# Experts' matmuls in two passes behind a branch on the token count, a gather of whole rows, and a share of the weight split for GpSimd

## The chip, the cores and the metric

The kernel runs on one core of a Trainium2 chip. The metric is the device time of one execution in microseconds: 1957.58 us, the median of three runs (1957.22 to 1958.94). The core has five engines that work side by side and wait for each other through semaphores: TensorE (PE, matmuls), VectorE (DVE), ScalarE (ACT), GpSimd (POOL) and SyncE (SP), which here only issues DMA transfers.

## The reference

Two encoder layers, each with a token mixer, a cross-attention and a channel mixer, over 256 tokens of width 1024, all in float32. The channel mixer of the second layer is a mixture of eight experts, and it is the part that the change touches:

```python
def moe_swiglu(x, w_router, w_gate, w_up, w_down):
    logits = (xt @ w_router).astype(jnp.float32)
    top_logit, top_e = lax.top_k(logits, TOP_K)          # TOP_K = 2 of 8
    top_w = jax.nn.softmax(top_logit, axis=-1)
    ...
    def expert_block(args):
        xs, e = args
        hdn = jax.nn.silu(xs @ w_gate[e]) * (xs @ w_up[e])
        return hdn @ w_down[e]
```

`w_gate[e]` and `w_up[e]` are 1024 x 3584, `w_down[e]` is 3584 x 1024. With the inputs given, the router sends 79, 52, 30, 59, 51, 63, 92 and 86 tokens to experts 0 to 7: five of the eight have at most 64.

## The kernel before

**Split numbers.** Every float32 operand is held as two parts, a high one `h` (the number rounded to the matmul's format) and a low one `l` (the rest). A product takes three passes on PE: high x high, high x low weights, low x high weights.

**Weights.** `wload` brings 1 MB of a weight (a piece: 128 partitions x 2048 columns) through SP's queue into a buffer `wr` (11 of them in the expert stage: 2 + 5 + `NX` = 3, and one more from the cross-attention), and takes it apart into `wh` and `wl`: ACT copies with rounding (`wh`, L312), and DVE subtracts (`wl = wr - wh`, L316). Outside the token mixer DVE does all of the subtraction, in `PX` = 4 parts of 512 columns in the expert stage. In the token mixer a part of the columns goes to POOL (L319). `wh` and `wl` live in a ring of 4 pairs of buffers.

**An expert.** `gather` takes the tokens of an expert into 128 slots: matmuls of `xtok` (both parts) against a selection `pd` give x^T of the expert in PSUM, and ACT copies it into `xg`. `expert_run` then walks 7 chunks of 512 hidden columns. For each, `gate_up` loads four pieces (gate twice, up twice) and runs 2 x 8 x 3 matmuls of 512 columns; SiLU on ACT and a product on DVE make `hs`. `down` of the chunk before follows: four transposes, the split into `hh` and `hl`, two pieces, and 24 matmuls into `ps_ye`. So a chunk has six pieces, an expert 42, and the stage 336 pieces and 8 x 504 such matmuls. `combine` adds the weighted result into `x`. Behind the stage a branch on the largest count (L1463) skips a second run for experts with over 128 tokens; it is skipped with these inputs.

**Order.** One program order, in which a scheduler of the tile framework moves instructions ahead where buffers allow. Each engine then works strictly in its own order. SP issues the loads in that order too; a load waits until DVE has read the last of what the buffer held.

Of the kernel before, what the change touches and what calls it, by code (L numbers as in the profile page):

```python
# [10 lines left out]
F32 = mybir.dt.float32  # L11
# [8 lines left out]
P = 128  # L20
# [17 lines left out]
PM, PC, PX = 2, 4, 4  # L38
# [6 lines left out]
NX = 3  # L45
# [13 lines left out]
GQ = 16  # L59
LEVELS = (16, 8, 4, 2, 1)  # L60
# [61 lines left out]
def _tiles():  # L122
    """name -> (index, first k-tile, k-tiles, first column, columns) of the pieces in which a weight is loaded"""
# [39 lines left out]
def tile_encoder(ctx: ExitStack, tc: tile.TileContext, a: dict, out: bass.AP, cw: dict):  # L163
# [95 lines left out]
    def load_rest(M):  # L259
# [10 lines left out]
        # lower bound of the second layer  # L270
# [19 lines left out]
    where = _offsets()  # L290

    def wload(name, i, k0, n0, c0, n1, late=()):
        """late: instructions behind which the parts are taken"""
# [8 lines left out]
        # behind a norm only the first weights may be split before it ends  # L302
# [3 lines left out]
        with ExitStack() as es:  # L306
# [3 lines left out]
            g = n * (GQ - GP[layer[0]]) // GQ if in_mixer[0] else n  # L310
            for s in (slice(j, j + c) for j in range(0, n, c)):
# [11 lines left out]
    def wload_halves(name, i, k0, n0, c0, n1, cols):  # L323
        """a piece of weights as two halves of its columns or of its k-tiles, in small buffers"""
# [19 lines left out]
    def together(*parts):  # L344
        """interleaves generators that yield the share of their work that is done"""
# [9 lines left out]
    def later(gen, n):  # L355
        """the steps of a generator as if they stood n instructions further down"""
# [13 lines left out]
    def proj_feat_steps(name, i, c0, ncol, xh, xl, evac, bank_=None):  # L370
        """out^T[f, tok]: weights stationary"""
# [38 lines left out]
    def rms_rstd(dst, ss, n, bias=None):  # L410
        """dst = (ss / n + eps) ** -0.5"""
# [15 lines left out]
    def log_sig(dst, src):  # L427
        """dst = ln(1 + exp(-src)) = -ln(sigmoid(src))"""
# [7 lines left out]
    def mixer(l, xh, xl, kctx):  # L436
        wi = ("w_in", l)
        with tc.tile_pool(name=f"mx{l}", bufs=1, reuse_waits="tile") as M, ExitStack() as mctx:
# [32 lines left out]
            def unit(f0, n):  # L471
                """l2 norm of the heads of conv tiles f0 .. f0 + n"""
# [10 lines left out]
            def products(w, f0):  # L483
                """k of a chunk against its tiles f0 .. f0 + 3, heads of either parity in a bank"""
# [11 lines left out]
            def A1():  # L496
# [28 lines left out]
                # (I + L^T)^-1 of the 32-blocks: 96 blocks side by side on the partitions  # L525
# [34 lines left out]
            def A1c(LT, wm):  # L560
# [37 lines left out]
            def A1b(beta, ld, DB):  # L598
# [38 lines left out]
            def A2(k_t, v_t, beta, ef, cdp, fb, AT, U64, col_b):  # L637
                # u', w'^T, k decays
# [37 lines left out]
                # state recurrence  # L676
# [30 lines left out]
                # outputs  # L707
# [76 lines left out]
            # C projections  # L784
# [97 lines left out]
    def softmax_rows(M, ps, n, scale, pt):  # L882
        """ps [P, n, 256] logits in PSUM -> pt [P, n, 256] probabilities"""
# [62 lines left out]
    def mixer_c(l, MS, big, c2, g2, M, sg, qc, ci, cg, oc):  # L946
# [27 lines left out]
        # chunk decays and the decayed queries  # L974
# [17 lines left out]
        # state recurrence  # L992
# [107 lines left out]
    def affine(e, x, mean, rstd, lp):  # L1100
        """x <- (x - mean) * rstd * gain + bias"""
# [168 lines left out]
    def moe(l, i, xh, xl, xth, xtl):  # L1270
        with weights("r3", NX, ring=raws), tc.tile_pool(name="mo", bufs=1, reuse_waits="tile") as O:
# [19 lines left out]
            # experts ahead of an expert: a larger logit, or the same one and a lower index  # L1291
# [35 lines left out]
            V.tensor_copy(cnti, cnt)  # L1327
            slot2 = sm("slot2")
# [3 lines left out]

            def gather(e, sl):
                pd = O.tile([P, NH, P], F32R, name="pd", tag="pd", bufs=2)
# [4 lines left out]
                for i, src in enumerate((xth, xtl)):  # L1339
                    for k0 in (0, 4):  # L1340
                        pg = bank(psb, "pb", "ps_gt").rearrange("p (k t) -> p k t", k=4)
                        for k in range(4):
                            for hf in range(NH):
                                T.matmul(pg[:, k], src[:, hf, (k0 + k) * P:(k0 + k + 1) * P], pd[:, hf],
                                         start=hf == 0, stop=hf == NH - 1)
                        A.activation(g[:, i, k0:k0 + 4], pg, AF.Copy)
                return g[:, 0], g[:, 1]
# [203 lines left out]
```

## Time and profile before

| | us |
|---|---|
| median of three timed runs | 1957.58 |
| span of the profiled execution (first to last instruction) | 1961.2 |
| first weight subtraction of the expert stage to the end of the last | 926.4 to 1936.5 |

The profiled execution gives no time of its own beside its span, which is 3.6 us over the median of the timed runs. In the views below a row of an engine carries the line of the kernel that made it, what it wrote and read, shapes and times. PE's matmuls are pipelined and their recorded durations overlap, so the distance from one start to the next is their pace.

### The profile page before, as it was taken

Reading aid. Unit: us, or ns where it says so; the run is one execution under the profiler, and the core shown is the slowest. Engines: PE = TensorE matmul, PEld = TensorE weight load, DVE = VectorE, ACT = ScalarE, POOL = GpSimd, SP = SyncE. Lnnn points to the kernel's source line nnn. Section 1 sums busy time; section 2 is a strip of 40 time slices with the busy share of each in tenths; the row PEclk is TensorE's granted clock in tenths of the full one; section 3 lists DMA queues with packets and bytes.
Section 4 is the critical chain, followed back from the end, with each engine's and each line's share of the span. In section 5 each row is a group of like instructions: output and inputs, shape, how many; then the busy total and the mean of one; then the engine's idle time right before and its main releaser. Section 6 shows DMA issues by size and latency. Waiting matters only on the chain. (4 is left out here: it accounts for less than half of the span.)

```text
span 1961.2 us, 31715 instructions
## 1 busy us (share of the span) xinstructions
PE 1838.9 (94%) x11906; PEld 1544.8 (79%) x11906; DVE 1575.2 (80%) x2812; ACT 1277.4 (65%) x2559; POOL 257.4 (13%) x248
## 2 busy tenths in 40 slices
PE   6889999999979898998999999999999999999996
PEld 5778779899967777686888788887888878788784
DVE  7887665755578966665889989899899898998986
ACT  4755435555536544454788778787877877787774
POOL 4545310000036353001000000000000000000000
PEclk8988999999989888998999999999999999999998
DMA  6321255555323313552999999999999989999980
GB/s 217 111 101 67 90 190 206 176 180 185 126 81 119 103 67 108 215 215 95 350 354 354 346 357 342 354 350 350 346 350 354 351 335 358 339 353 343 347 349 23
DMA packets 71266, 473.44 MB, mean 241 GB/s; under 512 B 8768, under 2 KB 12224, under 8 KB 15936
## 3 DMA queue, kind: packets, MB, share of 16 engines
q1 hardware_dynamic: 70384, 466.09, 64.6%
q10 hardware_dynamic: 720, 5.24, 0.7%
q8 instruction: 95, 1.56, 0.3%
q14 instruction: 67, 0.55, 0.1%
HBM read 470.26 MB, written 1.05 MB: 240 GB/s over the span
## 5 line engine op out<-in xcount | busy, mean ns | idle before, releaser
L316 DVE TENSOR_TENSOR wl<-wr,wh 128x512 fp32r<-128x512 f32 (+2 forms) x1622 | 1017.6, 693 | 119.3 <-ACT wh L312 116.8
L312 ACT ACTIVATE wh<-wr 128x512 fp32r<-128x512 f32 (+1 forms) x1656 | 915.0, 630 | 241.1 <-PE ps_gu L1365 152.2
L1364 PE MATMUL ps_gu<-wl,xg 128*128 128x512 f32 x896 | 352.8, 395 | 0.1
L1363 PE MATMUL ps_gu<-wh,xg 128*128 128x512 f32 x896 | 350.9, 397 | 0.0
L1365 PE MATMUL ps_gu<-wh,xg 128*128 128x512 f32 x896 | 350.6, 392 | 0.0
L1364 PEld LDWEIGHTS ps_gu<-wl,xg 128*128 128x128 f32 x896 | 169.0, 189 | 37.8 <-DVE wl L316 2.3
L1363 PEld LDWEIGHTS ps_gu<-wh,xg 128*128 128x128 f32 x896 | 169.1, 189 | 36.8 <-ACT wh L312 0.5
L1365 PEld LDWEIGHTS ps_gu<-wh,xg 128*128 128x128 f32 x896 | 168.8, 188 | 36.9
L1387 PE MATMUL ps_ye<-wh,hh 128*128 128x512 f32 x448 | 176.7, 396 | 4.6 <-ACT hh L408 4.6
L1388 PE MATMUL ps_ye<-wl,hh 128*128 128x512 f32 x448 | 176.6, 394 | 0.0
L1389 PE MATMUL ps_ye<-wh,hl 128*128 128x512 f32 x448 | 169.8, 397 | 0.0
L319 POOL TENSOR_TENSOR wl<-wr,wh 128x384 fp32r<-128x384 f32 (+6 forms) x68 | 103.6, 1544 | 290.4 <-ACT wh L312 290.1
L1475 POOL TENSOR_TENSOR x<-x,lp 128x512 f32<-128x512 f32 x1 | 1.8, 1817 | 1029.2 <-ACT x L1474 1029.2
L1387 PEld LDWEIGHTS ps_ye<-wh,hh 128*128 128x128 f32 x448 | 84.2, 188 | 26.7 <-ACT hh L408 7.9
L1257 PE MATMUL ps_gu<-xTl,wh 128*128 128x256 f32 x352 | 99.1, 282 | 0.0
L1388 PEld LDWEIGHTS ps_ye<-wl,hh 128*128 128x128 f32 x448 | 84.3, 188 | 18.6
L1256 PE MATMUL ps_gu<-xTh,wh 128*128 128x256 f32 x352 | 98.8, 282 | 0.0
L1258 PE MATMUL ps_gu<-xTh,wl 128*128 128x256 f32 x352 | 98.8, 281 | 0.0
L1389 PEld LDWEIGHTS ps_ye<-wh,hl 128*128 128x128 f32 x448 | 82.5, 188 | 17.3
L1257 PEld LDWEIGHTS ps_gu<-xTl,wh 128*128 128x128 f32 x352 | 66.7, 189 | 0.6 <-DVE xTl L408 0.2
L1256 PEld LDWEIGHTS ps_gu<-xTh,wh 128*128 128x128 f32 x352 | 66.7, 190 | 0.5
L1258 PEld LDWEIGHTS ps_gu<-xTh,wl 128*128 128x128 f32 x352 | 66.8, 190 | 0.0
(451 smaller groups left out, 3276.9 us busy)
## 6 DMA issues: line engine op xcount, KB each, us to landing
wr<-in_moe_wg_dram SPq DMA_DIRECT2D x112, 1024.0 KB, 6.8
wr<-in_moe_wu_dram SPq DMA_DIRECT2D x112, 1024.0 KB, 6.9
wr<-in_moe_wd_dram SPq DMA_DIRECT2D x112, 1024.0 KB, 7.0
wr<-in_w_in_dram SPq DMA_DIRECT2D x16, 1024.0 KB, 4.9
wr<-in_ffn_wg_dram SPq DMA_DIRECT2D x11, 1024.0 KB, 5.2
wr<-in_ffn_wu_dram SPq DMA_DIRECT2D x11, 1024.0 KB, 5.0
wr<-in_ffn_wd_dram SPq DMA_DIRECT2D x11, 1024.0 KB, 4.9
wr<-in_xk_dram SPq DMA_DIRECT2D x8, 1024.0 KB, 4.9
```

The lines of the kernel that those rows point to most:

```text
L312: A.activation(h[:, s], raw[:, s], AF.Copy)
L316: V.tensor_sub(l[:, m], raw[:, m], R_(h[:, m]))
L319: G.tensor_sub(l[:, m], raw[:, m], R_(h[:, m]))
L1256: T.matmul(ps[:, g], wh[:, k, fs], xh[:, k, :], start=k == 0, stop=False)
L1257: T.matmul(ps[:, g], wh[:, k, fs], xl[:, k, :], start=False, stop=False)
L1258: T.matmul(ps[:, g], wl[:, k, fs], xh[:, k, :], start=False, stop=k == KT - 1)
L1363: T.matmul(pt, gh[:, k], wh[:, k4], start=k == 0, stop=False)
L1364: T.matmul(pt, gh[:, k], wl[:, k4], start=False, stop=False)
L1365: T.matmul(pt, gl[:, k], wh[:, k4], start=False, stop=k == KT - 1)
L1387: T.matmul(ye[n], hh[:, f0 + f], dh[:, f, ns], start=b, stop=False)
L1388: T.matmul(ye[n], hh[:, f0 + f], dl[:, f, ns], start=False, stop=False)
L1389: T.matmul(ye[n], hl[:, f0 + f], dh[:, f, ns], start=False, stop=z)
```

## The change

Three edits, all in the expert stage, and three constants (`PX` 4 to 2, `NX` 3 to 2, `XPOOL` = 640).

1. *Two passes.* Where an expert has at most 64 tokens, the 64 upper slots of its stationary operand, empty otherwise, hold the low parts of the 64 lower ones (`halves_of`). Two passes then give all three products (and low x low), the upper 64 rows holding the low part's share. For gate and up these rows are folded onto the lower ones by one more matmul with a shifted identity (`fold`), for which ACT copies the product out of PSUM (`fe`); for down, `combine` adds the two rows by its selection matrix. The count is read into a PE register, and each of the 28 groups of products of an expert is written twice, with three passes and with two, behind a compare-and-branch on PE. The copies and folds run for all experts.
2. *Gather of whole rows.* The selection `pd` is stationary, the tokens stream in 512 columns, both parts into one bank; ACT copies the rows out, PE transposes them, and they are split anew.
3. *GpSimd.* Of the 2048 columns of an expert's piece DVE subtracts 1408 (1024 and 384) and POOL 640.

```diff
-PM, PC, PX = 2, 4, 4
+PM, PC, PX = 2, 4, 2
-NX = 3
+NX = 2
+HALF = P // 2
+XPOOL = 640
...
             g = n * (GQ - GP[layer[0]]) // GQ if in_mixer[0] else n
+            if name.startswith("moe"):
+                g = n - XPOOL
...
+            def halves_of(h, l, e):
+
+                t = O.tile([P, 4, HALF], F32, name="t")
+                V.tensor_scalar(t, R_(h)[:, :, HALF:], few[:, 1, e:e + 1], None, op0=OP.mult)
+                V.scalar_tensor_tensor(h[:, :, HALF:], R_(l)[:, :, :HALF], few[:, 0, e:e + 1], t, op0=OP.mult, op1=OP.add)
...
+                many = nc.tensor.value_load(cnti[0:1, e:e + 1], min_val=0, max_val=S) if packs else None
...
+                for n in range(2):
+                    ns = slice(n * 512, n * 512 + 512)
+                    pg = bank(psb, "pb", "ps_gr")
+                    for i, src in enumerate((xth, xtl)):
+                        for hf in range(NH):
+                            T.matmul(pg, pd[:, hf], src[:, hf, ns], start=i + hf == 0, stop=i + hf == NH)
+                    rows = O.tile([P, 512], F32, name="rows", tag="fe", bufs=2)
+                    A.activation(rows, pg, AF.Copy)
...
+                def products(many, ws, h, l):
+
+
+                    def passes(three):
+                        for j, (out, k, wh, wl, b, z) in enumerate(ws):
+                            T.matmul(out, h[:, k], wh, start=b, stop=False)
+                            T.matmul(out, h[:, k], wl, start=False, stop=z and not three)
+                            if three:
+                                T.matmul(out, l[:, k], wh, start=False, stop=z)
+                    if many is None:
+                        passes(True)
+                        return
+                    with tc.If(many > HALF) as c:
+                        passes(True)
+                    with c.Else():
+                        passes(False)
...
+                    if many is not None:
+                        for pt in pgu:
+                            fe = O.tile([P, 512], F32R, name="fe", tag="fe", bufs=2)
+                            A.activation(fe, pt, AF.Copy)
+                            T.matmul(pt, fold[e], fe, start=False, stop=True, skip_group_check=True)
```

DVE, in the middle of the expert stage, before: `wl<-wr,wh` are the weight subtractions (four to a piece), `hs` and `hl` the chunk's own work on what PE left in PSUM, `pd` the selection of the next expert.

```order
L316 TENSOR_TENSOR wl<-wr,wh 128x512 x24
L1369 TENSOR_TENSOR hs<-hs,ps_gu 128x512
L408 TENSOR_TENSOR hl<-ps_hT,hh 128x512
L316 TENSOR_TENSOR wl<-wr,wh 128x512 x8
L408 TENSOR_TENSOR hl<-ps_hT,hh 128x512
L316 TENSOR_TENSOR wl<-wr,wh 128x512 x16
L1369 TENSOR_TENSOR hs<-hs,ps_gu 128x512
L316 TENSOR_TENSOR wl<-wr,wh 128x512 x20
```

DVE at such a place now:

```order
L412 TENSOR_TENSOR hl<-ps_hT,hh 128x512
L1346 TENSOR_SCALAR t<-hh,few 128x256
L1353 TENSOR_SCALAR pd<-consts,slot 128x128 x2
L1392 UNCONDITIONAL_BRANCH
L1347 SCALAR_TENSOR_TENSOR hh<-hl,few,t 128x4x64
L320 TENSOR_TENSOR wl<-wr,wh 128x1024
L320 TENSOR_TENSOR wl<-wr,wh 128x384
```

A piece now has two subtractions on DVE, of 1024 and 384 columns, and the two instructions of `halves_of` have come in (72 of each in the stage).

POOL at the entry of the expert stage, before: the low part of the tokens is its last work until the branch behind the stage (L1446 reads the count for it).

```order
L1106 TENSOR_SCALAR x<-x,mv 128x512
L1107 TENSOR_TENSOR x<-x,lp 128x512
L1108 TENSOR_TENSOR x<-x,lp 128x512
L1215 TENSOR_TENSOR xtokl<-x,xtokh 128x1024 x2
L1446 TENSOR_LOAD cnti
```

POOL at the same place now:

```order
L1111 TENSOR_TENSOR x<-x,lp 128x512
L1112 TENSOR_TENSOR x<-x,lp 128x512
L1219 TENSOR_TENSOR xtokl<-x,xtokh 128x1024 x2
L323 TENSOR_TENSOR wl<-wr,wh 128x640 x4
L1392 UNCONDITIONAL_BRANCH x2
L323 TENSOR_TENSOR wl<-wr,wh 128x640 x3
```

From here POOL has 336 subtractions of 640 columns, one to a piece, where it had none.

PE at a chunk's end, before: the gate product of the next chunk and the down product stand mixed.

```order
L1364 MATMUL ps_gu<-wl,xg 128x512
L1365 MATMUL ps_gu<-wh,xg 128x512
L1375 MATMUL ps_hT<-consts,hs 128x128 x4
L1389 MATMUL ps_ye<-wh,hl 128x512 x2
L1387 MATMUL ps_ye<-wh,hh 128x512
L1388 MATMUL ps_ye<-wl,hh 128x512
```

PE at such a place now:

```order
L1392 UNCONDITIONAL_BRANCH
L1414 MATMUL ps_gu<-fe,fold 128x512 x2
L1392 COMPARE_AND_BRANCH
L1385 MATMUL ps_ye<-wh,hh 128x512
L1386 MATMUL ps_ye<-wl,hh 128x512
L1388 MATMUL ps_ye<-wh,hl 128x512
```

The products now stand in closed groups between branches, twice each, and the folds stand between the groups. The other engines get an unconditional jump at each of the 224 places.

## Rows read from the trace of the kernel before

**Rows 1.** The page's busy times: us, share of the span, instructions.
```profile
PE 1838.9 (94%) x11906; PEld 1544.8 (79%) x11906; DVE 1575.2 (80%) x2812; ACT 1277.4 (65%) x2559; POOL 257.4 (13%) x248
```

**Rows 2.** Busy us by stretch: PE, PEld, DVE, ACT, POOL, PE clock, DMA share, GB/s.
```profile
920.00:940.00 20.00, 16.25 (x74) 14.51 (x72) 15.84 (x51) 11.30 (x23) 2.76 (x2) 0.65 0.60 222
926.40:1936.50 1010.10, 1005.37 (x4603) 824.32 (x4604) 920.29 (x1537) 796.50 (x1506) 0.00 (x0) 0.99 0.91 339
1460.00:1480.00 20.00, 19.52 (x88) 15.41 (x87) 19.96 (x35) 14.89 (x28) 0.00 (x0) 1.00 0.91 340
1860.00:1880.00 20.00, 20.00 (x91) 16.38 (x90) 19.11 (x33) 16.26 (x30) 0.00 (x0) 1.00 1.01 408
```

**Rows 3.** Groups by line, 926.4 to 1936.5: busy us, mean ns | idle before, releasers.
```profile
L316 DVE TENSOR_TENSOR wl<-wr,wh 128x512 fp32r<-128x512 f32 x1344 | 827.8, 685 | 76.3 <-ACT wh L312 74.3 <-DMA wr<-in_moe_wd_dram 1.2
L312 ACT ACTIVATE wh<-wr 128x512 fp32r<-128x512 f32 x1330 | 718.1, 620 | 178.3 <-PE ps_gu L1365 152.2 <-PE ps_ye L1389 24.1 <-ACT hh L408 0.8
L1364 PE MATMUL ps_gu<-wl,xg 128*128 128x512 f32 x896 | 352.8, 395 | 0.1
```

**Rows 4.** Waits of SP's queue: us in total, times, longest.
```profile
SPq L298 <- DVE wl L316: 1321.0, 404, 24.7
```

**Rows 5.** PE in order of time, first and last of a run: start, us.
```profile
1404.52 0.39 PE L1363 MATMUL ps_gu<-wh,xg 128*128 128x512 f32 x1
...
1407.24 0.60 PE L1375 MATMUL ps_hT<-consts,hs 128*128 128x128 f32 x4
```

**Rows 6.** DVE in order of time, first and last weight subtractions of the stage.
```profile
926.40 2.49 DVE L316 TENSOR_TENSOR wl<-wr,wh 128x512 fp32r<-128x512 f32 x4
...
1935.17 1.29 DVE L316 TENSOR_TENSOR wl<-wr,wh 128x512 fp32r<-128x512 f32 x2
```

**Rows 7.** DVE in order of time, in the first layer's mixer.
```profile
26.22 0.47 DVE L460 SCALAR_TENSOR_TENSOR kvs<-cpad,cwt,kvs 128x256 f32<-128x256 f32 x1
26.62 2.96 DVE L316 TENSOR_TENSOR wl<-wr,wh 128x640 fp32r<-128x640 f32 x1
...
43.93 2.75 DVE L513 TENSOR_TENSOR rd<-ld,cmix 128x384 f32<-128x384 f32 x1
...
140.25 0.69 DVE L336 TENSOR_TENSOR hl<-wr,hh 128x512 fp32r<-128x512 f32 x1 [3.21 <-issue]
```

**Rows 8.** POOL in order of time, the same stretches and two more.
```profile
26.41 2.49 POOL L319 TENSOR_TENSOR wl<-wr,wh 128x1024 fp32r<-128x1024 f32 x1 [0.39 <-ACT wh L312]
...
42.22 4.05 POOL L319 TENSOR_TENSOR wl<-wr,wh 128x384 fp32r<-128x384 f32 x2 [5.03 <-ACT wh L312]
...
78.22 1.02 POOL L319 TENSOR_TENSOR wl<-wr,wh 128x384 fp32r<-128x384 f32 x1
...
120.24 2.53 POOL L337 TENSOR_TENSOR hl<-wr,hh 128x384 fp32r<-128x384 f32 x1 [3.65 <-ACT hh L335]
...
140.29 1.80 POOL L337 TENSOR_TENSOR hl<-wr,hh 128x512 fp32r<-128x512 f32 x1 [3.01 <-issue]
```

**Rows 9.** One line's instructions (L460): ns min/median/max, first and last start.
```profile
L460 DVE SCALAR_TENSOR_TENSOR kvs<-cpad,cwt,kvs x48: 471/478/2059, 18.4 to 612.8; 128x256 f32<-128x256 f32 x48
```

**Rows 10.** Groups by line and shape, ACT, 240 to 935.
```profile
L312 ACT ACTIVATE wh<-wr 128x1024 fp32r<-128x1024 f32 x18 | 18.0, 1054 | 6.0 <-PE ps_gu L1257 4.2 <-PE ps_f L385 1.8
L408 ACT ACTIVATE xTh<-ps_xT 128x512 fp32r<-128x512 f32 x20 | 11.9, 595 | 23.9 <-PE ps_xT L1135 18.0 <-DVE x L1104 2.8 <-issue 2.8
```

**Rows 11.** Instructions of L1463 (the branch behind the experts) and L1446.
```profile
L1463 PEldq EVENT_SEMAPHORE  x2: 51/51/51, 1945.9 to 1946.0; - x2
...
L1463 POOLq COMPARE_BRANCH  x1: 45/45/45, 936.5 to 936.5; - x1
L1463 POOLq EVENT_SEMAPHORE  x1: 17/17/17, 936.7 to 936.7; - x1
...
L1463 PEldq COMPARE_BRANCH  x1: 3555/3555/3555, 1942.3 to 1942.3; - x1
...
L1446 PEldq TENSOR_LOAD <-cnti x1: 486/486/486, 1941.7 to 1941.7; - x1
```

More of the change, by code (lines that the diff above doesn't have):

```diff
@@ L1327, in moe @@
             V.tensor_copy(cnti, cnt)
+            few = O.tile([P, 2, NE], F32, name="few")
+            V.tensor_scalar(few[:, 0], cnt[:, 0:NE], HALF + 0.5, None, op0=OP.is_lt)
+            V.tensor_scalar(few[:, 1], few[:, 0], -1.0, 1.0, op0=OP.mult, op1=OP.add)
+            upper = O.tile([P, P], F32, name="upper")
+            V.tensor_scalar(upper, iotas, HALF - 0.5, -float(HALF), op0=OP.is_gt, op1=OP.mult)
             slot2 = sm("slot2")
@@ L1337, in gather @@
                 pd_end.append(i)
+                many = nc.tensor.value_load(cnti[0:1, e:e + 1], min_val=0, max_val=S) if packs else None
                 g = act.tile([P, 2, KT, P], F32R, name="xg", tag="opTh" if e % 2 == 0 and sl is slot else "opTl")
[L1339 to L1347, printed above, removed]
+                for n in range(2):
[6 more added lines that the diff above has]
+                    A.activation(rows, pg, AF.Copy)
+                    pg = bank(psb, "pb", "ps_gt").rearrange("p (k t) -> p k t", k=4)
+                    for k in range(4):
+                        T.transpose(pg[:, k], rows[:, k * P:(k + 1) * P], ident)
+                    ks = slice(4 * n, 4 * n + 4)
+                    evac_split(g[:, 0, ks], g[:, 1, ks], pg)
+                    if packs:
+                        halves_of(g[:, 0, ks], g[:, 1, ks], e)
+                return g[:, 0], g[:, 1], many
             def expert_run(experts, sl, late=False):
@@ L1352, in expert_run, with gate_up @@
                 pend = []
-                def gate_up(e, gh, gl, c, late=False):
+                def products(many, ws, h, l):
[12 more added lines that the diff above has]
+                        passes(False)
+                def gate_up(e, gh, gl, many, c, late=False):
                     pgu = []
@@ L1357, in gate_up @@
                         pt = abank("ps_gu")
+                        todo = []
                         for kh in range(2):
@@ L1362, in gate_up @@
                                 k = kh * 4 + k4
[L1363 to L1365 removed]
+                                todo.append((pt, k, wh[:, k4], wl[:, k4], k == 0, k == KT - 1))
+                        products(many, todo, gh, gl)
                         pgu.append(pt)
+                    if many is not None:
[3 more added lines that the diff above has]
+                            T.matmul(pt, fold[e], fe, start=False, stop=True, skip_group_check=True)
                     hs = O.tile([P, 512], F32, name="hs", tag="hs", bufs=HSB)
@@ L1370, in gate_up, with down @@
                     return hs
-                def down(e, c, hs, ye):
+                def down(e, many, c, hs, ye):
                     pT = bank(psb, "pb", "ps_hT").rearrange("p (f t) -> p f t", f=4)
@@ L1378, in down @@
                     ends = evac_split(hh, hl, pT)
+                    if many is not None:
+                        halves_of(hh, hl, e)
                     for f0 in (0, 2):
@@ L1386, in down, with combine @@
                                 ns = slice(n * 512, n * 512 + 512)
-                                T.matmul(ye[n], hh[:, f0 + f], dh[:, f, ns], start=b, stop=False)
-                                T.matmul(ye[n], hh[:, f0 + f], dl[:, f, ns], start=False, stop=False)
-                                T.matmul(ye[n], hl[:, f0 + f], dh[:, f, ns], start=False, stop=z)
-                def combine(e, ye, first):
+                                todo.append((ye[n], f0 + f, dh[:, f, ns], dl[:, f, ns], b, z))
+                        products(many, todo, hh, hl)
+                def combine(e, many, ye, first):
                     pg = O.tile([P, NH, P], F32, name="pg", tag="pd", bufs=2)
+                    cols = iotas
+                    if many is not None:
+                        cols = O.tile([P, P], F32, name="cols")
+                        V.scalar_tensor_tensor(cols, upper, few[:, 0, e:e + 1], iotas, op0=OP.mult, op1=OP.add)
                     for hf in range(NH):
-                        V.tensor_scalar(pg[:, hf], iotas, sl[:, hf, e:e + 1], None, op0=OP.is_equal)
+                        V.tensor_scalar(pg[:, hf], cols, sl[:, hf, e:e + 1], None, op0=OP.is_equal)
                     pT = bank(psb, "pb", "ps_pT")
```

24 lines of the change are left out of this document (15 added, 9 removed).

## The prediction

> **What bounds the kernel now.** The page's busy times come first [rows 1]: PE 94%, DVE 80%, but over the whole span. So the second view is by stretch, for the expert stage alone, from the first weight subtraction to the last [rows 6]: 1010 us, half of the execution, and the only part that the change touches. There PE has work in 1005.4 of 1010.1 us, DVE in 920, ACT in 797, and POOL in none [rows 2]. DMA is busy to 91% at 339 GB/s, and reaches 408 GB/s in its best stretch, so it is near its end, but not at it. That PE sets the pace the reader sees from who waits: ACT's 178 us of idle time before its rounding end with a matmul (PE gave a buffer of the ring back), DVE's 76 us with ACT, PE's own with nothing [rows 3], and SP's loads wait for DVE to empty a buffer, 1321 us in all [rows 4]. The chain runs PE, ring, ACT, DVE, load buffer. A run of twelve matmuls takes 2.72 us, 0.227 us each [rows 5], so the twelve of a piece 2.72 us of the 3.01 us that a piece has (1010.1 / 336), and DVE's four subtractions of it 2.49 us [rows 6].
>
> **PE: what the two passes take away.** Five experts drop a third of 504 matmuls: 168 x 0.227 = 38.1 us each, 191 us in all. The folds add 14 matmuls per expert, 3.2 us, to all eight. The gather swaps 32 matmuls of 128 columns for 8 of 512 and 8 transposes, which I take as even: 8 x 0.227 = 1.8 us, and the transposes as a third of that. An expert has 126.3 us now, so PE would need 129.5 us for one with many tokens and 91.4 us for one with few; by PE alone the stage would be 3 x 129.5 + 5 x 91.4 = 846 us, a gain of 165. The question is what comes next.
>
> **ACT and DMA.** ACT rounds a piece in two halves of 1.05 us instead of four of some 0.53 (718 us over the stage's pieces [rows 3, 10]), so nothing changes there; the copies for the folds add 14 x 0.6 per expert. 84 x 1.05 + 32 x 0.6 (fold, SiLU, hidden, gather) + 2 for the combination = 109 us. DMA has 352 MB to bring; at 339 / 0.91 = 373 GB/s that is 945 us, 118 us per expert. One load buffer less costs cover of 3 us, which matters only if DMA is late. Both lie below today's 126.
>
> **DVE and POOL: the term that decides.** Alone, DVE would now have 1024 + 384 columns of a piece, about 1.6 us, and POOL 640. But the mixer shows what happens when both subtract [rows 7, 8]. DVE's 640 columns, issued at 26.62, took 2.96 us: POOL's 1024 had begun at 26.41 and ended at 28.90, and DVE was done 0.68 us later. POOL's 512 columns, issued at 140.29, took 1.80 us: DVE's 512 ended at 140.94, and POOL was done 1.15 us after that. POOL's 384 columns take 1.02 us alone, and 2.53 us where they meet a row of DVE instructions. Neither ever runs while the other does, if both read two operands from SBUF, as every weight subtraction does. So their times add. The price behind a hand-over: DVE 0.41 us for 384 (POOL ends at 46.27, DVE at 46.68), 0.68 for 640, so 1.05 ns a column, and 1.08 for 1024. POOL 1.15 for 512 and 2.21 for 1024 (from 26.69, where DVE ended, to 28.90), so 2.07 ns a column, and 1.42 for 640. A DVE instruction behind another has 0.60 for 512 (from 2.49 for four [rows 6]), so 0.47 for 384. **A piece: 1.42 + 1.08 + 0.47 = 2.97 us**, where DVE alone took 2.49. All 336: 998 us. The second instruction of `halves_of` reads two operands from SBUF too: 72 x 0.3 (0.28 behind POOL, 0.47 alone [rows 9]) = 22 us. The pair needs 1020 us, 10 more than the stage has now, whatever PE saves. DVE's work on PSUM (`hs`, `hl`) fits beside POOL.
>
> [...]
>
> **How tight the pair packs.** Between 0.5% idle, what PE loses now as the bounding engine [rows 2], and 9%, what DVE idles now (90 us of 1010). I take 2%, 20 us, near PE's row: ACT, at 109 of 130 us, can keep four buffers of the ring ahead. The last piece ends later: 0.47 + 1.42 behind ACT's last half, instead of one subtraction of 0.69, +1 us. An error of 0.05 us in a piece is 17 us.
>
> **Branches.** Far jumps are dear: PE's over the second experts' code took 3.56 us [rows 11]. POOL's at the same branch, over a few dozen instructions, was followed by its next instruction 0.2 us later [rows 11]; the new jumps pass 8 to 24 matmuls, so I take 0.2. On PE they run beside matmuls in flight, as the 0.49 us of the register load did at 1941.7 among matmuls. Below nothing they can't go; at 0.2 us uncovered, two per group, 28 groups, they'd be 11 us on each of three experts with many tokens, of which the pair's pace covers little. On the other engines they go past busy units.
>
> **Sum.** 10 + 20 + 1 = +31 us. The profiled span is 1961.2, so 1992; the timed runs lie 3.6 us lower, so **1989 us**.
>
> **The rivals.** (a) *Not slower: the port is no bound*, because subtractions on the two sides overlap more than the mixer's rows let think. Then few-token experts go at DMA's 118 us, the others at PE's 129.5: 3 x 129.5 + 5 x 118 = 978, -32, so 1926 us. It decides from a piece's cost of 2.9 us downwards. Against it: every pair of rows that I read. For it: DMA and ACT both have room. (b) *No change*: 2.92 us a piece and no idle time give 981 + 22 = 1003 us, -7, and with the 0.5% and the tail -1: 1957. (c) *Jumps cost a fetch each.* One of 3.56 us in each of 28 groups: 129.5 + 99.7 = 229 us for many tokens, 191 for few, so 3 x 229 + 5 x 191 = 1642, +632, 2590 us. From 1.4 us a group (the 39 us between 91 and 130, over 28) it overtakes the pair in experts with few tokens. Against it: POOL's 0.2. [...]
>
> [...]
>
> [...]
>
> **How the numbers follow.** Forecast (slower, 1962 to 2040): 0.62. Rival (b): 0.10. Rival (a): 0.18, half of it above 1930. (c): 0.07. (d): 0.03. The range must hold 0.80: 1930 to 2040 takes the forecast nearly whole, (b), and half of (a); the upper end is 5% idle and 0.08 us more a piece. About 0.2%, 4 us, is what a measurement can tell from no change. Faster 0.18, same 0.10, slower 0.72.
>
> **What would show it.** Right: in the expert stage DVE's subtractions last far beyond 1.2 us where POOL is at work, POOL's 640 columns take 1.4 to 3 us, DVE and POOL together fill 97% of the stage and PE waits for `wl` of either, at 17.8 us and more a chunk in experts of both kinds. SP waits for POOL. Wrong: chunks of 16.5 us with few tokens, DMA at 0.98 (rival a); PE's sequencer with long compare-and-branch rows (c).

## The result and the profile after

The changed kernel takes 2162.18 us (median of four runs, 2157.84 to 2166.52) against 1958.26, a ratio of 1.1038 (95% interval 1.1018 to 1.1057): 204 us slower, where 31 were forecast. The direction and the bound were as forecast, the size was not. The page after, line for line beside [rows 1]:

```profile
PE 1786.2 (83%) x11050; PEld 1430.5 (66%) x11050; DVE 1768.6 (82%) x2327; ACT 1261.4 (58%) x1999; POOL 930.5 (43%) x584
```

By stretch (columns as in [rows 2]): the expert stage from its first weight subtraction on DVE to its last, a run of chunks within an expert with 30 tokens, that expert's end with the next one's start, and the expert with 92 tokens.

```profile
925.80:2128.40 1202.60, 957.84 (x3737) 713.96 (x3738) 1107.90 (x1050) 780.04 (x951) 668.24 (x332) 0.91 0.80 286
1282.00:1402.00 120.00, 92.34 (x347) 65.69 (x346) 113.29 (x106) 83.84 (x104) 76.84 (x36) 0.90 0.86 307
1402.00:1429.00 27.00, 18.82 (x63) 13.87 (x62) 22.09 (x26) 14.08 (x18) 12.34 (x7) 0.81 0.76 279
1844.00:1998.50 154.50, 137.31 (x576) 108.18 (x576) 141.89 (x130) 99.09 (x122) 85.52 (x43) 0.94 0.80 282
```

The stage grew from 1010.1 to 1202.6 us, 192.5 of the 197.6 by which the span grew. PE lost its place as the bound (957.8 of 1202.6, 80%, where it had 99.5%), DMA fell from 339 to 286 GB/s, and DVE is the busiest engine. In steady chunks it is busy for 113.3 of 120 us. From one expert's combination to the next's (the first `yh` of each), the five experts with few tokens take 146 to 149 us and the one with 92 tokens 154: of the 38 us that two passes take from PE in an expert, 5 to 8 are seen.

Groups by line and shape in the stage (columns as in [rows 3]):

```profile
L323 POOL TENSOR_TENSOR wl<-wr,wh 128x640 fp32r<-128x640 f32 x332 | 668.2, 2023 | 535.8 <-ACT wh L316 383.1 <-DVE wl L320 38.2 <-DMA wr<-in_moe_wd_dram 32.3
...
L320 DVE TENSOR_TENSOR wl<-wr,wh 128x1024 fp32r<-128x1024 f32 x336 | 536.4, 1597 | 37.5 <-ACT wh L316 37.2
L320 DVE TENSOR_TENSOR wl<-wr,wh 128x384 fp32r<-128x384 f32 x336 | 400.1, 1191 | 0.0
...
L1347 DVE SCALAR_TENSOR_TENSOR hh<-hl,few,t 128x256 fp32r<-128x256 f32 x56 | 52.5, 938 | 0.9
```

The mean, the number after the busy time, is what to read. DVE's 384 columns last 1191 ns, hardly less than its 1024 columns last alone (1.21 us in the runs below without POOL). The halves (the second instruction of `halves_of`) last 938 ns, where 256 columns last 478 alone [rows 9]. So DVE is recorded as busy, but stands behind POOL for much of it. In order of time, DVE and then POOL:

```profile
1432.96 1.81 DVE L1347 SCALAR_TENSOR_TENSOR hh<-hl,few,t 128x256 fp32r<-128x256 f32 x1
1434.69 8.99 DVE L320 TENSOR_TENSOR wl<-wr,wh 128x384 fp32r<-128x384 f32 x6
...
1432.83 1.66 POOL L323 TENSOR_TENSOR wl<-wr,wh 128x640 fp32r<-128x640 f32 x1 [8.15 <-DMA wr<-in_moe_wd_dram]
1434.72 6.29 POOL L323 TENSOR_TENSOR wl<-wr,wh 128x640 fp32r<-128x640 f32 x3 [0.23 <-ACT wh L316]
```

The halves wait until POOL ends (1434.49) and end 0.28 us later. Then DVE's six subtractions (three pieces, 384 and 1024 by turns) and POOL's three fill 8.99 us, 3.00 a piece; the prediction had 2.97.

**The stage in three parts.** From start and duration of every DVE and POOL instruction in the trace, each moment of the stage falls into one of three. *Locked*: DVE runs an instruction with two operands in SBUF, or POOL runs any. *Other*: DVE runs something else (PSUM, one operand) and POOL nothing. *Idle*: neither runs. This is a way of counting; whether POOL holds DVE up is for the experiments. For the kernel after 1042.8 + 83.5 + 76.3 = 1202.6 us; the prediction had 1020 + 0 + 20, and 1 for the tail. (Where POOL fills with zeros its fills are not counted.) All runs by the same working, in us; each ratio is to runs of the kernel before that were taken beside it (medians 1958 to 1962):

| kernel | us (median) | ratio to before | stage | locked | other | idle |
|---|---|---|---|---|---|---|
| before | 1958.3 | 1 | 1010.1 | 827.9 | 92.4 | 89.8 |
| after | 2162.2 | 1.104 | 1202.7 | 1042.8 | 83.5 | 76.3 |
| before + POOL's 640 | 2104.6 | 1.075 | 1153.6 | 1010.3 | 66.4 | 76.9 |
| before, two parts, one buffer less | 1966.1 | 1.002 | 1015.9 | 784.6 | 91.7 | 139.5 |
| after, POOL fills with zeros | 1904.4 | 0.971 | 947.7 | DVE 592.1 | 129.9 | 225.6 |
| after, three passes, no branch | 2155.0 | 1.100 | 1191.7 | 1043.1 | 96.3 | 52.4 |
| after, no folds | 2138.1 | 1.091 | 1180.4 | 1041.5 | 80.5 | 58.4 |
| after, POOL's columns first | 2131.2 | 1.088 | 1173.8 | 1044.0 | 60.0 | 69.9 |
| after, 256 columns | 2025.6 | 1.034 | 1067.2 | 910.1 | 79.7 | 77.5 |
| after, 0 columns | 2037.4 | 1.041 | 1081.1 | 812.2 | 121.7 | 147.1 |
| 0 columns, three passes | 2049.8 | 1.046 | 1094.1 | 816.6 | 124.0 | 153.5 |
| 0 columns, no folds | 1953.9 | 0.996 | 1000.2 | 811.3 | 119.1 | 69.9 |
| 0 columns, later folds | 2056.5 | 1.049 | 1101.4 | 812.2 | 122.3 | 166.9 |
| 0 columns, ring of five | 2041.6 | 1.042 | 1085.0 | 811.1 | 122.0 | 151.9 |
| 0 columns, one-step halves | 1999.8 | 1.021 | 1051.9 | 786.3 | 127.7 | 137.9 |
| the two former together | 1976.6 | 1.009 | 1023.3 | 787.0 | 126.7 | 109.6 |
| two passes for down alone | 1945.3 | 0.994 | 992.1 | 826.0 | 91.0 | 75.1 |
| no halves (fastest) | **1922.5** | **0.981** | 966.9 | 782.8 | 100.0 | 84.0 |
| fastest + 256 columns | 1969.2 | 1.004 | 1013.7 | 879.5 | 69.7 | 64.5 |
| fastest + 640 columns | 2091.2 | 1.066 | 1134.7 | 1010.6 | 72.5 | 51.5 |

### The profile page after: what moved, and what is told of

It reads as the page before. It is cut to its first block, busy times and chain, and to the rows that moved or that the text cites. A ratio compares the mean times of both kernels' runs of the same rounds, so it can differ in the third digit from the quotient of the medians.

```text
span 2158.8 us, 30578 instructions
## 1 busy us (share of the span) xinstructions
PE 1786.2 (83%) x11050; PEld 1430.5 (66%) x11050; DVE 1768.6 (82%) x2327; ACT 1261.4 (58%) x1999; POOL 930.5 (43%) x584
## 5 line engine op out<-in xcount | busy, mean ns | idle before, releaser
L320 DVE TENSOR_TENSOR wl<-wr,wh 128x384 fp32r<-128x384 f32 (+4 forms) x950 | 1091.3, 1203 | 79.4 <-ACT wh L316 78.8
L323 POOL TENSOR_TENSOR wl<-wr,wh 128x640 fp32r<-128x640 f32 (+6 forms) x404 | 778.0, 1938 | 828.1 <-ACT wh L316 675.1
L316 ACT ACTIVATE wh<-wr 128x1024 fp32r<-128x1024 f32 (+2 forms) x984 | 854.7, 933 | 106.7 <-PE ps_gu L1261 22.7
L1386 PE MATMUL ps_gu<-wl,xg 128*128 128x512 f32 x896 | 390.7, 436 | 73.1 <-DVE wl L320 65.5
L1385 PE MATMUL ps_gu<-wh,xg 128*128 128x512 f32 x896 | 382.8, 427 | 3.9 <-DVE t L1346 3.9
L1385 PEld LDWEIGHTS ps_gu<-wh,xg 128*128 128x128 f32 x896 | 184.1, 205 | 39.6 <-DVE t L1346 4.3
L412 ACT ACTIVATE hh<-ps_hT 128x512 fp32r<-128x512 f32 x56 | 33.6, 600 | 210.4 <-PE ps_hT L1423 210.4
L1388 PE MATMUL ps_gu<-wh,xg 128*128 128x512 f32 x336 | 135.1, 402 | 0.0
L1416 ACT ACTIVATE hs<-ps_gu 128x512 f32<-128x512 f32 x56 | 33.4, 597 | 150.7 <-PE ps_gu L1414 150.7
L1423 PE MATMUL ps_hT<-consts,hs 128*128 128x128 f32 x224 | 36.6, 286 | 66.2 <-DVE hs L1417 63.1
L1388 PEld LDWEIGHTS ps_gu<-wh,xg 128*128 128x128 f32 x336 | 65.9, 196 | 14.6
L1388 PE MATMUL ps_ye<-wh,hl 128*128 128x512 f32 x168 | 68.8, 410 | 0.0
```

The source lines that it names most:

```text
L316: A.activation(h[:, s], raw[:, s], AF.Copy)
L320: V.tensor_sub(l[:, m], raw[:, m], R_(h[:, m]))
L323: G.tensor_sub(l[:, m], raw[:, m], R_(h[:, m]))
L412: return A.activation(h, ps, AF.Copy), V.tensor_sub(l, ps, R_(h))
L1385: T.matmul(out, h[:, k], wh, start=b, stop=False)
L1386: T.matmul(out, h[:, k], wl, start=False, stop=z and not three)
```

## Experiments: is it POOL's share?

**No columns for POOL, in the kernel after.**

```diff
-XPOOL = 640
+XPOOL = 0
```

> The kernel after, with GpSimd's share of a piece of experts' weights set to 0 columns, so that DVE subtracts all 2048 in two instructions of 1024. Theory P (the pair DVE and POOL shares a way to SBUF and sets the pace): the two instructions cost 2 x 1.21 = 2.42 us, 336 pieces 814 us, DVE's other work in the stage 152 us as in the trace after, and idle time of 20 to 83 us: a stage of 986 to 1049 us, and 948 us outside of it, so 1934 to 1997 us. Theory S (the longer serial chain of folds, halves, branches and the new gather holds every engine up, and the share of POOL is a side matter): POOL had free time in the stage, so little changes, over 2100 us.

**The share alone, in the kernel before.**

```diff
-PM, PC, PX = 2, 4, 4
+PM, PC, PX = 2, 4, 2
...
+            if name.startswith("moe"):
+                g = n - 640
```

> The kernel before, with nothing changed but the split of a piece of experts' weights: two parts of 1024 columns instead of four of 512, and the last 640 columns subtracted by POOL. No two passes, no folds, no new gather, no branches. Theory P: a piece costs the pair 2.97 us, 336 pieces 998 us, and of DVE's other 84 us between none and all lies beside POOL; with 20 to 83 us of idle time the stage has 1018 to 1165 us, so 1966 to 2113 us, slower than before. Theory S: PE still sets the pace, DVE is relieved, 1950 to 1965 us, no change.

**Three passes everywhere, no branch; and the same with no columns.**

```diff
-V.tensor_scalar(few[:, 0], cnt[:, 0:NE], HALF + 0.5, None, op0=OP.is_lt)
+V.tensor_scalar(few[:, 0], cnt[:, 0:NE], -1.0, None, op0=OP.is_lt)
...
-                    with tc.If(many > HALF) as c:
-                        passes(True)
-                    with c.Else():
-                        passes(False)
+                    passes(True)
```

> The kernel after, with three passes in every expert and no branch (the flag for few tokens is off, so the halves and the folds do their work on zeros and the result is the same). Theory P: experts with few tokens took as long as those with many (145 to 149 us against 148 to 155), PE has room for 38 us more in each of five, so within 1.5% of the kernel after, 2130 to 2195 us. Theory S: every group of products is a link of the chain, and becomes half as long again in five experts, 2200 to 2350 us. A cost of the branches themselves would show as a gain against the kernel after.

> Both of the former together: no columns for POOL, three passes everywhere and no branch; of the change the folds, halves, new gather and smaller number of parts are left. Theory P: PE needs 129.5 us for each of eight experts, 1036 us, and DVE 966 us, so a stage of 1040 to 1080 us and 1988 to 2028 us: above the run without columns for POOL by what two passes are worth. Theory S: over 2100 us, as the chain is unchanged.

The share alone makes the kernel before 146 us slower (1.0752, 1.0715 to 1.0788), inside theory P. Taking it away from the kernel after gives back 125 us, but leaves 79 (1.0405, 1.0376 to 1.0435): outside P's range and S's, so there is a second loss. Three passes everywhere cost nothing while POOL works (2155, inside theory P; 7 us less than the kernel after, with the branches gone): the 191 us that two passes take from PE are worth nothing behind this pair. Without POOL's share they are worth 12.5 us, and the time with three passes, 2050, again lies outside both theories.

**POOL's queue or the way to SBUF?** POOL does something else in the same place:

```diff
-                    G.tensor_sub(l[:, m], raw[:, m], R_(h[:, m]))
+                    if name.startswith("moe"):
+                        G.memset(l[:, m].bitcast(F32), 0.0)
+                    else:
+                        G.tensor_sub(l[:, m], raw[:, m], R_(h[:, m]))
```

> The kernel after, but POOL fills its 640 columns of a piece of experts' weights with zeros in place of subtracting (so these columns lack their low part, and the result lacks that product). DVE keeps 1024 and 384 columns. Theory P (the two sides exclude each other, and that is what POOL's share costs): a fill reads nothing and did not hold DVE up in the trace before, so a piece costs DVE 1.21 + 0.55 = 1.76 us, 336 of them 591 us, its other work 152 us, 743 in all; PE's 846 us and DMA's 352 MB at 415 GB/s, 848 us, bound the stage, and with stalls of 5 to 15% it has 890 to 975 us: 1838 to 1923 us. Rival W (the third party itself costs: a buffer is ready only when a third engine has run its part, late in its queue): a fill is in POOL's queue just so, over 2050 us.

1904.4 us, inside theory P. By the instructions that write `wl` (ns min/median/max, first and last start), the kernel after first, then this one:

```profile
L320 DVE TENSOR_TENSOR wl<-wr,wh x672: 543/1217/2612, 925.8 to 2127.9; 128x1024 fp32r<-128x1024 f32 x168
...
L323 POOL TENSOR_TENSOR wl<-wr,wh x336: 1533/1870/8086, 917.4 to 2126.1; 128x640 fp32r<-128x640 f32 x168
```

```profile
L320 DVE TENSOR_TENSOR wl<-wr,wh x672: 540/884/1228, 924.5 to 1871.6; 128x1024 fp32r<-128x1024 f32 x168
...
L324 POOL MEMSET wl<- x334: 626/633/827, 920.8 to 1860.9; 128x640 f32 x167
```

Beside POOL's fills none of 672 subtractions lasts over 1228 ns, what 1024 columns last alone; beside its subtractions they last up to 2612. A fill is also shorter (633 ns against 1533 at least), so the time alone doesn't part theory P from POOL's slowness; the durations on DVE do. Without POOL's subtractions, the two passes show (columns as in [rows 2], the experts with 30 and with 92 tokens):

```profile
1188.00:1298.10 110.10, 97.02 (x408) 73.53 (x408) 92.64 (x133) 97.76 (x122) 26.83 (x43) 0.97 0.99 404
1617.60:1753.60 136.00, 129.64 (x577) 103.62 (x576) 88.10 (x127) 100.26 (x124) 26.58 (x43) 1.00 0.90 343
```

**Price by column, or one collision per instruction?** 256 columns; and POOL's columns taken from the first half of a piece:

```diff
-XPOOL = 640
+XPOOL = 256
```

> The kernel after with 256 columns for POOL in place of 640. Theory L (the price is per column, and the times add): a piece costs 0.59 for POOL's 256 columns, 1.08 and 0.81 for DVE's 1024 and 768, 2.48 us, hardly more than the 2.42 of DVE alone; in proportion to the columns the loss of 125 us becomes 50: 2055 to 2090 us. Rival I (each of POOL's instructions costs one collision, whatever its size): 336 of them as before, 2120 to 2165 us.

```diff
+                if name.startswith("moe"):
+                    m = slice(max(s0, XPOOL), s1)
+                    V.tensor_sub(l[:, m], raw[:, m], R_(h[:, m]))
+                    if s0 == 0:
+                        m = slice(0, XPOOL)
+                        G.tensor_sub(l[:, m], raw[:, m], R_(h[:, m]))
+                    continue
```

> The kernel after with POOL's 640 columns taken from the first half of a piece (columns 0 to 640; DVE 640 to 1024, then the second half whole), so that POOL can begin 1 us earlier, while ACT is at the second half. Theory L, in step: the sum of both is the same, 2.97 us a piece, and DVE's 384 columns now meet POOL's 640 instead of its 1024 doing so: within 1.5% of the kernel after, 2130 to 2195 us. Rival T (POOL's late end is the loss, since PE waits for the last of three parts): 2080 to 2120 us.

The locked time grows with the columns, not with the instructions: 812.2, 910.1 and 1042.8 us for 0, 256 and 640. A column that goes from DVE to POOL adds 97.9 / (336 x 256) = 1.14 ns, and 230.6 / (336 x 640) = 1.07 ns, so on POOL it takes about twice the locked time that it took on DVE. The total at 256 columns (2025.6) lies below the 2055 from which theory L's range began, and even 12 us below 0 columns: idle time fell from 147 to 78 and other time from 122 to 80, together more than the 98 us that the locked time grew. Why idle time fell was not tried. With POOL first the locked time is the same (1044.0) and the run is 31 us faster: 102 us of POOL's time now lie beside DVE's other work, where 68 did, and other time fell by 23 of the 29 us by which the stage fell. So where POOL's part stands beside DVE's work is a part of the loss. The total, 2131, lies 1 us inside L's range and 11 above T's, so it does not part these two.

## Experiments: the second loss

**Constants, folds, later folds.**

```diff
-PM, PC, PX = 2, 4, 4
+PM, PC, PX = 2, 4, 2
...
-NX = 3
+NX = 2
```

> The kernel before with two of the constants of the change and nothing else: pieces of experts' weights in two parts of 1024 columns instead of four of 512, and one load buffer less. Theory K (the constants are part of what the run without columns for POOL still lost, 79 us): ACT's part of 1.05 us holds a short job of its queue up twice as long as one of 0.53, and one buffer less is 3 us less cover: 1970 to 2020 us. Rival F (the loss is all in folds and halves, which stand between PE, ACT and DVE once more per chunk): 1950 to 1962 us, no change.

```diff
-                    if many is not None:
+                    if False:
                         for pt in pgu:
                             fe = O.tile([P, 512], F32R, name="fe", tag="fe", bufs=2)
```

> The kernel after without columns for POOL, and without the folds and their copies (so experts with few tokens lack the low part of tokens against the gate and up weights). Theory F: in the run without columns for POOL PE's weight loads waited 78 us for the copies ahead of the folds, and its matmuls 65 us; without them the stage loses that much and ACT's 66 us of copies: 1945 to 1985 us. Rival K (constants, halves and gather): 2015 to 2040 us.

```diff
-                        hs = gate_up(e, gh, gl, many, c, late and n + c == 0)
+                        pgu = gate_up(e, gh, gl, many, c, late and n + c == 0)
                         if pend:
                             flush()
+                        hs = finish(e, many, pgu)
```

(`finish` is the second half of `gate_up`, from the folds on; its definition is left out here.)

> The kernel after without columns for POOL, with all its work, but the two folds of a chunk stand behind the down products of the chunk before instead of ahead of them, so that PE has 16 or 24 matmuls (3.6 or 5.4 us) to do while ACT copies. Theory F: PE's waits for the copies (78 us) go, and those for halves of the hidden part hardly change: 1950 to 1990 us. Rival K: 2015 to 2040 us.

> The kernel after with POOL's 640 columns, but without the folds and their copies (experts with few tokens lack the low part of tokens against the gate and up weights). Theory A (two losses that add: the pair of DVE and POOL, and the folds): the folds cost 83 us without POOL's share, so 2065 to 2095 us. Rival M (the pair alone sets the pace in the kernel after, so that folds cost there only what stands between its pieces): 2120 to 2160 us.

The last of these is the kernel after with POOL's 640 columns and the same edit as above, the folds left out. The constants cost 5 us (1.0023, 1.0006 to 1.0041), which lies between theory K and rival F. The folds cost 83 us without POOL's share (1953.9 against 2037.4, theory F) and 24 with it (2138.1 against 2162.2), where the pair is late anyway (rival M). So without the folds nothing of the 79 us is left; the new gather was never taken out by itself. What PE's weight loads waited for, with 0 columns (us in total, times, longest):

```profile
PEld ps_gu L1414 <- ACT fe L1413: 78.0, 33, 4.4
PEld ps_hT L1423 <- DVE hs L1417: 55.4, 30, 4.0
PEld ps_ye L1385 <- DVE hh L1347: 43.8, 16, 6.2
```

A copy of 0.59 us makes PE wait up to 4.4: it stands in ACT's queue behind roundings of weights. One such place in the run with 0 columns, ACT and then PE in order of time:

```profile
1355.92 0.59 ACT L1416 ACTIVATE hs<-ps_gu 128x512 f32<-128x512 f32 x1
1356.40 2.00 ACT L316 ACTIVATE wh<-wr 128x1024 fp32r<-128x1024 f32 x2
1358.29 0.60 ACT L1413 ACTIVATE fe<-ps_gu 128x512 fp32r<-128x512 f32 x1
...
1358.94 0.79 PE L1414 MATMUL ps_gu<-fe,fold 128*128 128x512 f32 x1 [3.31 <-ACT fe L1413]
```

Moving the folds behind the down products in the program's text did not cure it: the scheduler moved only some of them (60 of 112 folds had no down product between them and the last gate or up product, then 44 of 110 recorded), the waits stayed at 77.8 us, and the time rose by 19, above theory F and rival K. So this run doesn't test whether an earlier copy would help.

**A deeper ring, halves in one step.**

```diff
-        with weights("r3", NX, ring=raws), tc.tile_pool(name="mo", bufs=1, reuse_waits="tile") as O:
+        with weights("c3", 1), tc.tile_pool(name="mo", bufs=1, reuse_waits="tile") as O:
```

> The kernel after without columns for POOL, all its work, and the ring of high and low parts of weights five pairs deep instead of four, for two load buffers less. Theory R (a copy for a fold comes late in ACT's queue, PE stands still for it, gives back no pair of the ring, and ACT and DVE stand still in turn; a fifth pair bridges it): of the 153 us in which DVE is idle half goes, 1950 to 1990 us. Rival C (the order itself is the loss, each engine waits for the one ahead whatever the depth, or the two buffers less make the loads late): 2025 to 2060 us.

```diff
-                t = O.tile([P, 4, HALF], F32, name="t")
-                V.tensor_scalar(t, R_(h)[:, :, HALF:], few[:, 1, e:e + 1], None, op0=OP.mult)
-                V.scalar_tensor_tensor(h[:, :, HALF:], R_(l)[:, :, :HALF], few[:, 0, e:e + 1], t, op0=OP.mult, op1=OP.add)
+                V.scalar_tensor_tensor(h[:, :, HALF:], R_(h)[:, :, HALF:], few[:, 1, e:e + 1], l[:, :, HALF:], op0=OP.mult, op1=OP.add)
```

(`l` is here the product in PSUM, `few[:, 1]` minus the flag. The edits that put the tokens into both halves of the slots, in the selection and in the fold, are left out here.)

> The kernel after without columns for POOL, with the halves made in one instruction in place of two: the gather and the folds put the tokens of an expert with few into both halves of the slots, so that the low part of the upper half is PSUM minus the high part. DVE loses 72 x (0.34 + 0.48 - 0.40) = 30 us of work. If DVE's work sets the pace: 2000 to 2015 us. If waits between engines do: 2025 to 2045 us.

> The two former together: the halves in one instruction, the ring five pairs deep, no columns for POOL. By theory R and with DVE near its bound 1930 to 1960 us, about what the kernel before takes or less; by rival C 2020 to 2050 us.

A fifth pair alone gives nothing (2041.6 against 2037.4; theory R falls). The halves in one step give 38 us (two runs, 1995 and 2004), more than the 30 us that were estimated for DVE's work: locked and other time together fell by 20 us, idle time by 9 in the profiled executions. Behind them the fifth pair gives 23 more (1976.6), between what theory R and rival C gave; why it helps only there was not tried.

**No halves at all.** With the tokens in both halves of the slots, the high part of the upper and the low part of the lower half stand side by side in one buffer, and are the operand of the two passes without any work:

```diff
-                    hh = O.tile([P, 4, P], F32R, name="hh", tag="hh", bufs=2)
-                    hl = O.tile([P, 4, P], F32R, name="hl", tag="hl", bufs=2)
-                    ends = evac_split(hh, hl, pT)
-                    if many is not None:
-                        halves_of(hh, hl, e)
+                    hh = O.tile([P, 4, 2 * P], F32R, name="hx", tag="hx", bufs=2)
+                    ends = evac_split(hh[:, :, 0:P], hh[:, :, P:2 * P], pT)
...
+                            s0 = 0 if three else HALF
-                            T.matmul(out, h[:, k], wh, start=b, stop=False)
+                            T.matmul(out, h[:, k, s0:s0 + P], wh, start=b, stop=False)
...
```

The first of two kernels does so for the down product alone, in the kernel before, and needs no folds; the second, of which the cut above is a part, for all products, in the kernel after with 0 columns and five pairs. It keeps the folds.

> The kernel before with two passes for the down product alone, for experts with at most 64 tokens, and with no folds, no halves, no columns for POOL: the selection puts the tokens of such an expert into both halves of the slots, so that the rows 64 to 127 of the product of gate and up repeat the first 64; the high part of the upper and the low part of the lower half then stand side by side in one buffer, and are the stationary operand of the two passes as they are. DVE and ACT get no new work but one instruction per expert; PE loses 56 matmuls x 7 x 0.227 / 7 = 12.7 us in each of five experts and gains 12 branches of it. One load buffer less. If PE sets the pace as in the kernel before: 1958 - 64 = 1894 at best; with DVE at 920 us and 4 to 6% idle a stage of 957 to 979 us, 1905 to 1927 us. If the branches cost or the schedule is disturbed as with the folds: 1955 to 2000 us.

> The kernel after without columns for POOL, with two passes for all products, folds, and a ring of five pairs, but with the halves taken away as work: tokens in both halves of the slots, high and low parts side by side in one buffer. DVE has 814 + 84 + 15 = 913 us, ACT 66 us for the copies ahead of the folds. Without folds such a kernel would have 70 us of idle time on DVE as the run without folds had, with them 110 as the run with one instruction for the halves and five pairs: a stage of 983 to 1023 us, 1931 to 1971 us, around the kernel before. Below 1930 it would show that the halves, by their place between DVE and PE, cost more than their work.

Both beat the kernel before: two passes for the down product alone 0.9935 (0.9918 to 0.9952), all of them without halves and without POOL **1922.5 us, 0.9813 (0.9796 to 0.9829)**. The first, at 1945 us, lies between its two forecasts and gains 14 of the 64 us that PE saves at best. The second is below 1930, the mark that was set: against the one-step halves with five pairs it gains 54 us, half of it DVE's own work (locked and other time, 31 us less) and half idle time (26 less). That fits a cost of the halves by their place, too. And with its folds it has 84 us of idle time, so the 83 us of the folds above are not their price in every kernel. The second, by stretch: the stage, the expert with 59 tokens, the one with 92, and two chunks of the one with 59:

```profile
928.60:1895.50 966.90, 879.75 (x3749) 672.75 (x3750) 882.81 (x905) 773.90 (x951) 0.00 (x0) 0.98 0.91 358
1305.40:1415.70 110.30, 98.66 (x408) 72.00 (x408) 110.30 (x116) 97.42 (x122) 0.00 (x0) 0.97 0.99 401
1637.80:1775.30 137.50, 129.63 (x577) 105.25 (x576) 111.20 (x112) 100.30 (x124) 0.00 (x0) 0.99 0.87 330
1339.40:1369.00 29.60, 27.20 (x119) 20.73 (x120) 29.60 (x29) 26.85 (x34) 0.00 (x0) 1.00 1.01 421
```

With few tokens DVE and DMA are now both full, 110 us an expert; with many PE is near its end, 137.

**The share again, in this kernel.**

> The faster kernel (two passes, tokens in both halves of the slots, no halves, a ring of five pairs) with POOL's share put back to 640 columns. Theory L: the two engines' subtractions fill 1010 us as in the kernel before with the share alone (no halves, so none of their 33 us), DVE's work beside PSUM adds the 60 to 85 us that did not lie beside POOL in the other runs, and 60 to 80 us are idle: a stage of 1130 to 1175 us, 2078 to 2123 us. Rival S (the share costs only where the chain of halves and folds is slow): below 2000 us.

> The same faster kernel with 256 columns for POOL. In the other runs 256 columns added 105 us of locked time to DVE's 808 and took 77 us from DVE's subtractions' own, and cost nothing (2026 against 2037 us without). Theory L: no gain where DMA (14.8 us a chunk) and PE (18.4 us) set the pace, and a loss of some us where DVE is late: 1915 to 1945 us. Rival: a small share relieves DVE where it is late, at the start of an expert: 1895 to 1915 us.

640 columns cost 169 us (2091.2), as theory L had it; the locked time is that of the kernel before with the share, 1010.6 and 1010.3, and rival S falls. 256 columns cost 47 us, more than either theory gave: locked time rose by 97, other and idle time together fell by 50.

## The prediction, step by step

- **PE's part held for many tokens.** Such an expert was put at 129.5 us of PE; 129.6 are recorded in the two runs shown above in which PE is busy for 94 to 95% of it. One with few tokens was put at 91.4; 97.0 and 98.7 are recorded there, at a granted clock of 0.97, so 31 to 33 us are saved and not 38. They were there to be had, but not behind the pair.
- **The piece held.** 2.97 us were forecast and 3.00 measured; 998 us became 1010.3, and the halves' 22 us some 32 (1042.8 less 1010.3). Rival (d), that whole instructions add, falls: with the lone times of 1.53 us for POOL's 640 columns (the least in the kernel after), 1.21 for DVE's 1024 and 0.54 for its 384 (the least beside the fills), a piece would have 3.28 us.
- **"DVE's work on PSUM fits beside POOL" failed: 83.5 us instead of 0.** POOL does not hold the work on PSUM up: of the 56 `hs` in the kernel after 19 lie wholly beside a subtraction of POOL and take 0.67 to 0.69 us, as do the 31 with none beside them. But of DVE's 152 us of work of that kind (PSUM, or one operand) only 68 lay beside POOL. Of the 83.5, 47 are `hs` and `hl`, which the prediction named, and 14 the first instruction of the halves, which it did not. POOL gets its part of a piece when DVE gets its own (383 us of its idle time end with ACT's rounding), so it has often nothing left when DVE turns to PSUM. With POOL's columns first the 68 us rose to 102, and the time fell by 31.
- **"How tight the pair packs" failed: 76 us of idle time instead of 20.** I took PE's idle share, 0.5%, as the near row, because PE was the bound. DVE's own row stood beside it, 90 us of 1010 [rows 2]. DVE still waits for others when it sets the pace: in the kernel after 31 us for PE before `hs`, 22 for PE before the combination's `x`, and 37 for ACT's rounding. In all runs with POOL's 640 columns DVE and POOL were both idle for 52 to 77 us. The sign that the pair would fill 97% of the stage failed with it: 94%. 83.5 + 56 + 23 us make 162 of the 173 by which the forecast was short; 11 remain: 5 lie outside the stage, and the rest is in the main that the runs' median lies 3.4 us above the profiled span, where before it lay 3.6 below.
- **Folds at nothing in the sum was wrong, too**, but small here: 24 of the 204 us, which lie inside the terms above. Without POOL's share it would have been the main loss, 83 us.
- **The branches cost what was taken.** PE's compare-and-branch rows in the kernel after (ns min/median/max):

```profile
L1392 PEldq COMPARE_BRANCH  x308: 65/202/448, 936.7 to 2130.8; - x154
```

  No row is near the 3.56 us of the far jump [rows 11], in which the trace has one packet of an instruction queue (0.02 MB); the longest of the 308 has 0.45 us, and the kernel without branches is only 7 us faster: rival (c) falls.
- **Rivals (a) and (b) fall** with the measured time. What (a), subtractions that overlap, would have given is near what the run with fills shows: 1904, where 1926 was worked out. The difference is in the main DMA: with few tokens it moved 401 to 404 GB/s over an expert, not the 373 that I took.
- **The clock.** The sum took PE at 0.227 us a matmul throughout. The granted clock was 0.91 over the stage and 0.81 from 1402 to 1429, at an expert's start. Just ahead of that, behind a wait of 3.65 us, PE in order of time:

```profile
1395.38 0.51 PE L1386 MATMUL ps_gu<-wl,xg 128*128 128x512 f32 x1 [3.65 <-POOL wl L323]
1395.72 0.40 PE L1385 MATMUL ps_gu<-wh,xg 128*128 128x512 f32 x1
1395.96 0.40 PE L1386 MATMUL ps_gu<-wl,xg 128*128 128x512 f32 x1
...
1396.65 0.62 PE L1386 MATMUL ps_ye<-wl,hh 128*128 128x512 f32 x1
1397.08 0.63 PE L1385 MATMUL ps_ye<-wh,hh 128*128 128x512 f32 x1
1397.50 0.63 PE L1386 MATMUL ps_ye<-wl,hh 128*128 128x512 f32 x1
...
1400.06 0.40 PE L1386 MATMUL ps_ye<-wl,hh 128*128 128x512 f32 x1
1400.30 0.39 PE L1385 MATMUL ps_ye<-wh,hh 128*128 128x512 f32 x1
```

  Behind the wait the starts come to lie 0.24 us apart, then 0.43 for 3.4 us (granted clock 0.50 from 1396.65 to 1400.06), then 0.24 again. What that adds to the time was not separated.

**What stays open.** Why the copies for the folds cost 83 us without POOL's share (77 of it idle time of DVE), while neither a deeper ring nor another place in the text cured it; and why 256 columns gained 12 us in one kernel and cost 47 in another. The locked time grew alike (98 and 97 us); it was other and idle time that fell by 112 in the one and by 50 in the other.

## What to carry to other kernels

Work given to an engine that holds up the one it should relieve is no relief: here every column moved added 1.1 ns of locked time, and only the smaller share of 256 columns ever gained anything, in one of two kernels. Where an engine becomes the bound, sum its whole in-order queue, with the work that "fits beside" and its own idle row from before, not the idle row of the old bound. By the rows of before that is 1020 + 92 + 90 = 1202 us, where 1203 were measured, so near partly by luck: DVE got 60 us of new work of that kind, and 68 did fit beside. A saving on the bounding engine is worth what the next engines leave: two passes for all products brought 2% only after POOL's share was taken back and the work that they needed (halves, on DVE) had been designed away.

## What the runs showed of the hardware

- Subtractions on POOL and DVE, all operands in SBUF, add up: 1.06 to 1.14 ns of locked time more per column moved, nearly the same at 256 and 640 columns and in two kernels. Beside POOL's fills of the same columns (633 ns) no DVE subtraction lasted over 1228 ns, what 1024 columns last alone. Work with one operand in SBUF was held up by POOL's subtractions, too: the first instruction of the halves took 0.33 to 0.35 us with none beside it, and up to 1.71. At 640 columns the share was a loss in every kernel, 105 to 184 us.
- DMA moved 421 GB/s over 30 us (the kernel without halves) and 404 over a whole expert of 110 us (POOL fills with zeros), where the best 20 us shown of before had 408 [rows 2].
